# Gated linear recurrence: near-key products and their splitting moved from GpSimd to VectorE, decays of a level merged into one product

## The chip, the cores and the metric

The kernel runs on one core of a Trainium2 chip. The metric is the time of one execution on the device in microseconds (us); the median of several is compared. Smaller is better.

## The reference

Two pre-norm residual layers over 512 tokens of width 1024, all in float32. The first mixes tokens by a gated linear recurrence (8 heads, 128 keys and 128 values each), the second by sparse attention; each is followed by a feed-forward layer with a short convolution. The change touches the recurrence alone:

```python
forget = lb + (1.0 - lb) * sigmoid(f)          # per head, key dimension and token
k = (1.0 - lb) * sigmoid(-f)
log_f = log(maximum(forget, TINY))
...
b = cumsum(log_f)                              # within a chunk of 32
decay = exp(b[t] - b[s]) for s <= t
scores = einsum('bhtd,bhsd,bhtsd->bhts', q, k, decay)
o = scores @ i + (q * exp(b)) @ S              # S: state carried from chunk to chunk
S = exp(b_last) * S + (k * exp(b_last - b)) @ i
...
out = (rms_norm(o) * gate_norm * silu(g)) @ w_out
```

## The kernel before, in words

All activations lie transposed, features on the 128 partitions and tokens along the columns. Every float32 matrix product of a projection is made of three products of a high and a low part (`split`: ScalarE copies the high part, VectorE subtracts it for the low one; `mm3` issues the three). A projection to 128 features (`proj_T`) is 24 such products of 512 columns into one PSUM bank `pj`; its weights (1024 columns after loading) are split into `whi` and `wlo` (L143, L144).

The recurrence (42 to 304.5 us of the profile) runs head by head. `fq(h)` projects f and q, `gate(h)` projects g, and `recur(h)` does the head's recurrence. `recur` is a generator that is woven into the projections: each `yield` names how much projection work is to come before it goes on. So TensorE's order is written out by hand through these yields, while a scheduler orders the other engines when the program is built; every engine then takes its instructions in that fixed order.

`recur(h)` computes the 512 x 512 scores of a head by doubling. Distances of 0, 1 and 2 to 3 tokens are products of columns, w: `q * k` (512 columns, L489), one set of 256 (L487) and two of 256 (L493, tiles `w[1]`, `w[2]`). They are split into `wh`/`wl` and summed over the partitions by products with ones into three banks `pd`; then copied into `Sd` under masks (L528 to L534). Each level m = 4, 8, ... 256 multiplies blocks of m keys with the neighbouring m queries into a bank `pl` (L544 to L556), after which `decay(m)` multiplies queries of the second blocks (`qf`, L506) and keys of the first ones (`k`, L508) by decay factors out of a tree (`ftree`, L512), so that blocks of 2m are ready. Levels 32 and 64 use a packed copy of k (`kc`, L563). At the end the scores multiply the values (`po`), the result is normalised by ScalarE and GpSimd, transposed (`pt`), gated by g (L610) and split into `oh`/`ol`.

GpSimd has the 256-column products of w, their low parts `wl`, the product `g = g * gs` (L471) and two small operations on norms.

A head's level 256 stands in TensorE's order shortly before the next head's `pd`: this is what is called a seam below. "Decay 128" is the call `decay(128)`.

## Time and profile before

| what | value |
| --- | --- |
| median of 3 executions | 1307.05 us (1306.79 to 1308.17) |
| profiled execution | 1307.64 us, of which its span 1305.9 us |
| TensorE busy | 1260.3 us, 97% |
| VectorE, ScalarE, GpSimd busy | 858.9, 578.7, 185.7 us |
| mean granted clock of TensorE | 0.991 of full speed |

Busy time of matmuls overlaps from one to the next, so a high share does not say that TensorE runs at its peak; what counts is where it has gaps, what ends them, and at what clock it runs. GpSimd works mostly in the recurrence and in the attention.

### The profile page before, as it was taken

How to read it: one execution, taken by the hardware profiler on the slowest of the kernel's cores; microseconds unless marked ns; L12 is line 12 of the kernel's file. 1: busy time of each engine (PE TensorE's matmuls, PEld its weight loads, DVE VectorE, ACT ScalarE, POOL GpSimd, SP SyncE). 2: the span in 40 equal slices, each digit the busy share in tenths (PEclk: the TensorE clock that was granted, in tenths of full speed). 3: DMA queues.
4: the chain of work that ended last, by engine and by line, in shares of the span. 5: the costliest groups of instructions: out<-in, count | busy, mean ns of one | idle time of the engine just before them, and what ended most of it. 6: DMA issues, size and time to landing. Idle time of an engine off the chain costs nothing.

```text
span 1305.9 us, 15769 instructions
## 1 busy us (share of the span) xinstructions
PE 1260.3 (97%) x6054; PEld 1050.5 (80%) x6054; DVE 858.9 (66%) x1354; ACT 578.7 (44%) x980; POOL 185.7 (14%) x159
## 2 busy tenths in 40 slices
PE   9999899989999999999999979999999999999997
PEld 7788677778888888888887867898888888888887
DVE  7765988875677777762434799964677777772331
ACT  5434344444444444431325556873444444441430
POOL 3313233330000000000003385220000000000000
PEclk9989999999999999999999999999999999999999
DMA  6322221112333333333235221101333333332222
GB/s 194 100 63 67 63 66 49 49 50 84 93 97 97 97 97 98 97 97 97 89 98 145 65 65 34 49 2 53 107 99 98 97 97 97 97 97 97 82 80 65
DMA packets 171099, 109.90 MB, mean 84 GB/s; under 512 B 4832, under 2 KB 160400, under 8 KB 171024
## 3 DMA queue, kind: packets, MB, share of 16 engines
q1 hardware_dynamic: 170320, 108.31, 28.0%
q8 instruction: 47, 0.77, 0.2%
q10 hardware_dynamic: 704, 0.58, 0.2%
q14 instruction: 28, 0.23, 0.1%
HBM read 106.76 MB, written 2.12 MB: 83 GB/s over the span
## 4 chain that ended last, share of the span: by engine, by line
PE 83%; DVE 9%; POOL 3%; issue 2%; ACT 2%; DMA 0%; POOLq 0%; DVEq 0%; SPq 0%; ACTq 0%
PE pj L161 15%; PE pj L162 15%; PE pj L163 15%; PE px L161 8%; PE px L163 8%; PE px L162 8%; PE pav L911 2%; PE pl L544 1%; PE po L590 1%; DVE scs L750 1%; PE pn L162 1%; PE pn L161 1%; PE pn L163 1%; PE pl L852 1%; POOL wl L144 1%
## 5 line engine op out<-in xcount | busy, mean ns | idle before, releaser
L161 PE MATMUL pj<-x,whi 128*128 128x512 f32 (+1 forms) x1016 | 403.5, 397 | 0.0
L162 PE MATMUL pj<-x,whi 128*128 128x512 f32 (+1 forms) x1016 | 396.6, 390 | 0.0
L163 PE MATMUL pj<-x,wlo 128*128 128x512 f32 (+1 forms) x1016 | 396.6, 390 | 0.0
L144 DVE TENSOR_TENSOR wlo<-wr,whi 128x1024 fp32r<-128x1024 f32 (+2 forms) x184 | 228.1, 1240 | 165.0 <-ACT whi L143 162.5
L143 ACT ACTIVATE whi<-wr 128x1024 fp32r<-128x1024 f32 (+3 forms) x194 | 201.9, 1041 | 283.6 <-PE px L162 155.3
L163 PEld LDWEIGHTS pj<-x,wlo 128*128 128x128 f32 (+1 forms) x1016 | 190.9, 188 | 40.9
L161 PEld LDWEIGHTS pj<-x,whi 128*128 128x128 f32 (+1 forms) x1016 | 191.3, 188 | 39.4 <-issue 1.6
L162 PEld LDWEIGHTS pj<-x,whi 128*128 128x128 f32 (+1 forms) x1016 | 191.3, 188 | 38.9 <-issue 1.0
L161 PE MATMUL px<-ah,whi 128*128 128x512 f32 (+1 forms) x332 | 128.5, 387 | 0.0
L163 PE MATMUL px<-ah,wlo 128*128 128x512 f32 (+1 forms) x332 | 127.5, 384 | 0.0
L162 PE MATMUL px<-al,whi 128*128 128x512 f32 (+1 forms) x332 | 126.2, 380 | 0.0
L340 DVE TENSOR_TENSOR ub<-pj,rstd_r 128x512 f32<-128x512 f32 x88 | 60.6, 688 | 82.5 <-PE pj L163 77.6
L143 ACT ACTIVATE ah<-c 128x512 fp32r<-128x512 f32 x44 | 27.8, 631 | 116.0 <-DVE c L352 116.0
L163 PEld LDWEIGHTS px<-ah,wlo 128*128 128x128 f32 x332 | 62.3, 188 | 13.5
L162 PEld LDWEIGHTS px<-al,whi 128*128 128x128 f32 x332 | 62.3, 188 | 12.8
L343 ACT ACTIVATE c<-ub,convc 128x512 f32<-128x512 f32 x88 | 71.2, 809 | 2.4 <-DVE ub L340 1.6
L161 PEld LDWEIGHTS px<-ah,whi 128*128 128x128 f32 x332 | 62.4, 188 | 11.4
L345 DVE SCALAR_TENSOR_TENSOR c<-ub,convc,c 128x512 f32<-128x512 f32 x88 | 66.1, 752 | 3.0
L344 DVE SCALAR_TENSOR_TENSOR c<-ub,convc,c 128x512 f32<-128x512 f32 x88 | 65.6, 746 | 0.0
L350 ACT ACTIVATE c<-c 128x512 f32<-128x512 f32 x44 | 27.8, 632 | 80.7 <-DVE c L345 80.6
L321 POOL TENSOR_TENSOR rstd_c<-ms,half 128x2 f32<-128x2 f32 x2 | 1.4, 698 | 360.6 <-DVE ms L320 360.6
L712 POOL MEMSET vf<- 128x1536 f32 x1 | 1.4, 1382 | 354.0 <-PE px L163 354.0
(226 smaller groups left out, 1849.4 us busy)
## 6 DMA issues: line engine op xcount, KB each, us to landing
wr<-in_ffn_w_up_dram SPq DMA_DIRECT2D x88, 512.0 KB, 3.8
wr<-in_ffn_w_down_dram SPq DMA_DIRECT2D x41, 512.0 KB, 3.7
wr<-in_hgrn_w_in_dram SPq DMA_DIRECT2D x30, 512.0 KB, 4.1
wr<-in_dsa_w_in_dram SPq DMA_DIRECT2D x14, 512.0 KB, 3.7
wr<-in_hgrn_w_out_dram SPq DMA_DIRECT2D x8, 512.0 KB, 3.5
wr<-in_dsa_w_out_dram SPq DMA_DIRECT2D x8, 512.0 KB, 3.8
back<-Z SPq DMA_DIRECT2D x4, 512.0 KB, 4.4
out_dram<-hT SPq DMA_DIRECT2D x4, 512.0 KB, 4.2
```

The lines of the kernel that those rows point to most:

```text
L143: nc.scalar.activation(dst_h, src, AF.Copy)
L144: lo.tensor_tensor(dst_l, src, dst_h.bitcast(F32), op=ALU.subtract)
L161: nc.tensor.matmul(o, ah, bh, start=start, stop=False)
L162: nc.tensor.matmul(o, ah, bl, start=False, stop=False)
L163: nc.tensor.matmul(o, al, bh, start=False, stop=stop)
L340: nc.vector.tensor_tensor(u[:, 2:], o, rows(), op=ALU.mult)
L343: nc.scalar.activation(c, u[:, 2:], AF.Identity, scale=cc[2], bias=cc[3])
L344: nc.vector.scalar_tensor_tensor(c, u[:, 1:T + 1], cc[1], c, op0=ALU.mult, op1=ALU.add)
L345: nc.vector.scalar_tensor_tensor(c, u[:, 0:T], cc[0], c, op0=ALU.mult, op1=ALU.add)
L350: nc.scalar.activation(g, g, AF.Silu)
L544: nc.tensor.matmul(pl[:, ts_], k[:, ts_], qf[:, ts_], start=True, stop=True)
L911: nc.tensor.matmul(o[:, :256], vf[:, s, kv, c], px[:, e, s * 256:s * 256 + 256], start=e == 0 and s == 0, stop=False)
```

## The change

In each head's `recur`:

- the 256-column products of w go from GpSimd to VectorE. The two sets for distances 2 and 3 become one product of 512 columns. All lie in one tile `w` of 1280 columns;
- `w` is split by one copy on ScalarE and one subtraction on VectorE, where there were three copies on ScalarE and three subtractions on GpSimd;
- `qf` and `k` lie in one tile `qk`, and one product on VectorE of 512 columns (`turned(m)` by `factors(.., m)`) replaces the two of 256 columns at the first split and at each level;
- the factor 1 - lb of k is moved to q, where it joins the multiplication by the norm, so k's own multiplication goes; the scale and bias of f go from VectorE to ScalarE;
- `decay(m)` and `kc` are issued ahead of the yield that follows the level's products instead of behind it;
- the buffer counts of the tiles `tmp`, `f` and `q` go from 3 to 2.

GpSimd keeps `g = g * gs` and the two small operations.

```diff
--- before.py
+++ after.py
@@ -202,7 +202,7 @@
         if n == 0:
             nc.scalar.activation(sqa, hT[:, n, :], AF.Square)
         else:
-            sq = pool.tile([P, T], F32, name="sq", tag="tmp", bufs=3) if pool else nrm.tile([P, T], F32, name="sq", bufs=1)
+            sq = pool.tile([P, T], F32, name="sq", tag="tmp", bufs=2) if pool else nrm.tile([P, T], F32, name="sq", bufs=1)
             nc.scalar.activation(sq, hT[:, n, :], AF.Square)
             (nc.gpsimd if pool else nc.vector).tensor_tensor(sqa, sqa, sq, op=ALU.add)
 
@@ -443,55 +443,66 @@
     def fq(h):
         hs = slice(h, h + 1)
         pf = yield from proj_T(w_in, D + h * P)
-        f = hw.tile([P, T], F32, name="f", bufs=3)
-        k = hw.tile([P, T], F32, name="k", bufs=3)
+        f = hw.tile([P, T], F32, name="f", bufs=2)
+        qk = hw.tile([P, 2, T], F32, name="qk", bufs=3)
 
         def forget():
-            fr = hw.tile([P, T], F32, name="fr", tag="tmp", bufs=3)
+            fr = hw.tile([P, T], F32, name="fr", tag="tmp", bufs=2)
             nc.vector.tensor_tensor(fr, pf, rows(), op=ALU.mult)
             nc.scalar.activation(f, fr, AF.Sigmoid)
-            nc.scalar.activation(k, fr, AF.Sigmoid, scale=-1.0)
-            nc.vector.tensor_scalar(f, f, omlb[:, hs], lb[:, hs], op0=ALU.mult, op1=ALU.add)
+            nc.scalar.activation(qk[:, 1, :], fr, AF.Sigmoid, scale=-1.0)
+            nc.scalar.activation(f, f, AF.Identity, scale=omlb[:, hs], bias=lb[:, hs])
             nc.vector.tensor_scalar(f, f, TINY, None, op0=ALU.max)
-            nc.vector.tensor_scalar(k, k, omlb[:, hs], None, op0=ALU.mult)
             if h == 0:
                 values_out()
 
         pq = yield from proj_T(w_in, h * P, hook={3: forget})
-        q = hw.tile([P, T], F32, name="q", bufs=3)
-        nc.vector.tensor_tensor(q, pq, rows(), op=ALU.mult)
-        heads[h] = [q, f, k]
+        q = hw.tile([P, T], F32, name="q", bufs=2)
+
+        nc.vector.scalar_tensor_tensor(q, pq, omlb[:, hs], rows(), op0=ALU.mult, op1=ALU.mult)
+        heads[h] = [q, f, qk]
 
     def gate(h):
         pg = yield from proj_T(w_in, 3 * D + h * P)
         g = hw.tile([P, T], F32, name="g")
         nc.vector.tensor_tensor(g, pg, rows(), op=ALU.mult)
-        gs = hw.tile([P, T], F32, name="gs", tag="tmp", bufs=3)
+        gs = hw.tile([P, T], F32, name="gs", tag="tmp", bufs=2)
         nc.scalar.activation(gs, g, AF.Sigmoid)
         nc.gpsimd.tensor_tensor(g, g, gs, op=ALU.mult)
         heads[h].append(g)
 
     def recur(h):
-        q, f, k = heads[h]
+        q, f, qk = heads[h]
+        qf, k = qk[:, 0, :], qk[:, 1, :]
         Sd = hw.tile([P, TT, P], F32, name="Sd")
         S1 = hw.tile([P, 2, P], F32, name="S1")
         S2 = hw.tile([P, 2, 256], F32, name="S2")
 
 
-        qf = hw.tile([P, T], F32, name="qf")
         nc.vector.tensor_tensor(qf, q, f, op=ALU.mult)
-        w = [hw.tile([P, T], F32, name=f"w{i}", tag="tmp", bufs=3) for i in range(3)]
+        w = hw.tile([P, 1280], F32, name="w", bufs=1)
         q2, k2, f2 = (a.rearrange("p (n two) -> p n two", two=2) for a in (qf, k, f))
         q4, k4 = (a.rearrange("p (n four) -> p n four", four=4) for a in (qf, k))
         ftree = hw.tile([P, T], F32, name="ftree")
-        nc.gpsimd.tensor_tensor(w[1][:, :256], k2[:, :, 0], q2[:, :, 1], op=ALU.mult)
+        nc.vector.tensor_tensor(w[:, :512], q, k, op=ALU.mult)
+        nc.vector.tensor_tensor(w[:, 512:768], k2[:, :, 0], q2[:, :, 1], op=ALU.mult)
+
+        def turned(m):
+
+            nb = T // (2 * m)
+            return bass.AP(tensor=qk.tensor, offset=qk.offset + m, ap=[list(qk.ap[0]), [T - m, 2], [2 * m, nb], [1, m]])
+
+        def factors(fv, m):
+
+            nb = T // (2 * m)
+            return bass.AP(tensor=fv.tensor, offset=fv.offset, ap=[list(fv.ap[0]), [1, 2], [2, nb], [0, m]])
+
+        nc.vector.tensor_tensor(turned(1), turned(1), factors(f, 1), op=ALU.mult)
         nc.vector.tensor_tensor(ftree[:, :256], f2[:, :, 0], f2[:, :, 1], op=ALU.mult)
-        nc.vector.tensor_tensor(w[0], q, k, op=ALU.mult)
-        nc.vector.tensor_tensor(q2[:, :, 1], q2[:, :, 1], f2[:, :, 0], op=ALU.mult)
-        nc.vector.tensor_tensor(k2[:, :, 0], k2[:, :, 0], f2[:, :, 1], op=ALU.mult)
-        for i, o in ((0, w[1][:, 256:]), (1, w[2][:, :256])):
-            nc.gpsimd.tensor_tensor(o.rearrange("p (n two) -> p n two", two=2), q4[:, :, 2:],
-                                    k4[:, :, i:i + 1].to_broadcast([P, P, 2]), op=ALU.mult)
+        nc.vector.tensor_tensor(w[:, 768:].rearrange("p (i n two) -> p i n two", i=2, two=2),
+                                q4[:, None, :, 2:].to_broadcast([P, 2, P, 2]),
+                                k4[:, :, :2].rearrange("p n i -> p i n")[:, :, :, None].to_broadcast([P, 2, P, 2]),
+                                op=ALU.mult)
         trees = [ftree[:, :256], 256]
 
         def decay(m):
@@ -500,24 +511,17 @@
                 return
             ft, off = trees
             nb = T // (2 * m)
-            fv = ft.rearrange("p (n two) -> p n two", two=2)
-            qv = qf.rearrange("p (n two m) -> p n two m", two=2, m=m)
-            kv = k.rearrange("p (n two m) -> p n two m", two=2, m=m)
-            nc.vector.tensor_tensor(qv[:, :, 1, :], qv[:, :, 1, :],
-                                    fv[:, :, 0:1].to_broadcast([P, nb, m]), op=ALU.mult)
-            nc.vector.tensor_tensor(kv[:, :, 0, :], kv[:, :, 0, :],
-                                    fv[:, :, 1:2].to_broadcast([P, nb, m]), op=ALU.mult)
+            nc.vector.tensor_tensor(turned(m), turned(m), factors(ft, m), op=ALU.mult)
             if 4 * m < T:
+                fv = ft.rearrange("p (n two) -> p n two", two=2)
                 nft = ftree[:, off:off + nb]
                 nc.vector.tensor_tensor(nft, fv[:, :, 0], fv[:, :, 1], op=ALU.mult)
                 trees[:] = [nft, off + nb]
 
-        wp = []
-        for i, n in enumerate((512, 512, 256)):
-            wh = hw.tile([P, n], F32R, name=f"wh{i}", bufs=1)
-            wl = hw.tile([P, n], F32R, name=f"wl{i}", bufs=1)
-            split(wh, wl, w[i][:, :n], nc.gpsimd)
-            wp.append((wh, wl))
+        wh = hw.tile([P, 1280], F32R, name="wh", bufs=1)
+        wl = hw.tile([P, 1280], F32R, name="wl", bufs=1)
+        split(wh, wl, w)
+        wp = [(wh[:, c], wl[:, c]) for c in (slice(0, 512), slice(512, 1024), slice(1024, 1280))]
         yield START if h else 6.0
         decay(2)
         pd = [bank("pd")[:, :n] for n in (512, 512, 256)]
@@ -555,13 +559,13 @@
                 for i in range(2):
                     nc.tensor.matmul(pl[:, i * 256:(i + 1) * 256], k[:, i * P:(i + 1) * P],
                                      qf[:, 256:], start=True, stop=True)
-            yield LEV
             decay(m)
             if m in (16, 32):
 
                 kc = hw.tile([P, 256], F32, name="kc")
                 nc.scalar.activation(kc.rearrange("p (n m) -> p n m", m=2 * m),
                                      k.rearrange("p (n two m) -> p n two m", two=2, m=2 * m)[:, :, 0, :], AF.Copy)
+            yield LEV
             if m in LEVELS:
                 nc.vector.copy_predicated(
                     Sd, masks[:, LEVELS.index(m), None, :].to_broadcast([P, TT, P]), plv)
```

TensorE's rows stand in the same order in both programs, but for the tiles' names and the line numbers. VectorE's order moves. The first place is the seam of one of the heads 4 to 6, from the weight split ahead of level 64's decay to the next weight split. Before (the three-dimensional shapes are those of the decays, 128x2x128 is decay 128; `ol` belongs to the head before, `g` with L468 to this head's gate):

```order
L144 TENSOR_TENSOR wlo<-wr,whi 128x1024
L506 TENSOR_TENSOR qf<-qf,ftree 128x4x64
L506 TENSOR_TENSOR qf<-qf,ftree 128x128x2
L610 SCALAR_TENSOR_TENSOR g<-pt,cols,g 128x512
L508 TENSOR_TENSOR k<-k,ftree 128x128x2
L144 TENSOR_TENSOR ol<-g,oh 128x512
L468 TENSOR_TENSOR g<-pj,rstd_r 128x512
L506 TENSOR_TENSOR qf<-qf,ftree 128x2x128
L508 TENSOR_TENSOR k<-k,ftree 128x2x128
L144 TENSOR_TENSOR wlo<-wr,whi 128x1024
```

and in the changed program, where L514 is the merged decay (its last two numbers tell the level, 128x2x4x64 is decay 64), L500 the first split's, L502 the product of 512 columns, L614 the old L610:

```order
L144 TENSOR_TENSOR wlo<-wr,whi 128x1024
L500 TENSOR_TENSOR qk<-qk,f 128x2x256
L514 TENSOR_TENSOR qk<-qk,ftree 128x2x4x64
L502 TENSOR_TENSOR w<-qk 128x512
L614 SCALAR_TENSOR_TENSOR g<-pt,cols,g 128x512
L514 TENSOR_TENSOR qk<-qk,ftree 128x2x128x2
L468 TENSOR_TENSOR g<-pj,rstd_r 128x512
L144 TENSOR_TENSOR wl<-w,wh 128x1280
L144 TENSOR_TENSOR ol<-g,oh 128x512
L514 TENSOR_TENSOR qk<-qk,ftree 128x2x2x128
L144 TENSOR_TENSOR wlo<-wr,whi 128x1024
```

Decay 128 stood behind `g` and now stands behind `g`, the 1280-column `wl` and `ol`; two decays of 256 columns became one of 512 each time.

The second place is the first two heads, from the second head's q (L462) to the first head's decay 4. Before:

```order
L462 TENSOR_TENSOR q<-pj,rstd_r 128x512
L482 TENSOR_TENSOR qf<-q,f 128x512
L528 TENSOR_TENSOR Sd<-pd,ident 128x512
L489 TENSOR_TENSOR w_550<-q,k 128x512
L490 TENSOR_TENSOR qf<-qf,f 128x256
L491 TENSOR_TENSOR k<-k,f 128x256
L532 COPY_PREDICATED Sd<-pairs,pd 128x256
L144 TENSOR_TENSOR wlo<-wr,whi 128x1024
L534 COPY_PREDICATED Sd<-pairs,pd 128x128x2
L506 TENSOR_TENSOR qf<-qf,ftree 128x64x4
L534 COPY_PREDICATED Sd<-pairs,pd 128x128x2
L508 TENSOR_TENSOR k<-k,ftree 128x64x4
```

and in the changed program, where L532 to L538 are the copies into `Sd`:

```order
L462 SCALAR_TENSOR_TENSOR q<-pj,omlb,rstd_r 128x512
L518 TENSOR_TENSOR ftree<-ftree 128x8
L144 TENSOR_TENSOR wlo<-wr,whi 128x1024
L482 TENSOR_TENSOR qk<-q,f 128x512
L487 TENSOR_TENSOR w<-q,qk 128x512
L488 TENSOR_TENSOR w<-qk 128x256
L532 TENSOR_TENSOR Sd<-pd,ident 128x512
L500 TENSOR_TENSOR qk<-qk,f 128x2x256
L536 COPY_PREDICATED Sd<-pairs,pd 128x256
L502 TENSOR_TENSOR w<-qk 128x512
L538 COPY_PREDICATED Sd<-pairs,pd 128x128x2
L514 TENSOR_TENSOR qk<-qk,ftree 128x2x64x4
```

The weight split now stands ahead of the second head's products, the products L488 and L502 stand among them, and decay 4 of the first head (128x2x64x4) stands before the last pair copy instead of around it.

## Rows read from the trace of the kernel before

**Rows 1.** The page's chain that ended last: shares of the span by engine.

```profile
PE 83%; DVE 9%; POOL 3%; issue 2%; ACT 2%; DMA 0%; POOLq 0%; DVEq 0%; SPq 0%; ACTq 0%
```

**Rows 2.** Table by stretch: length, busy of the engines, TensorE's granted clock, DMA.

```profile
42.00:118.00 76.00, 71.90 (x361) 59.93 (x360) 52.40 (x97) 31.73 (x73) 17.97 (x17) 0.96 0.26 77
118.00:154.00 36.00, 30.05 (x149) 23.89 (x147) 31.66 (x53) 13.07 (x25) 15.60 (x13) 1.00 0.20 59
154.00:241.10 87.10, 79.03 (x426) 66.50 (x426) 73.56 (x131) 38.65 (x97) 31.78 (x27) 0.98 0.19 55
241.10:304.50 63.40, 59.77 (x322) 50.31 (x323) 42.04 (x69) 25.55 (x72) 16.35 (x15) 0.97 0.18 57
304.50:338.00 33.50, 33.50 (x147) 26.90 (x146) 23.70 (x31) 16.23 (x23) 0.19 (x4) 1.00 0.31 90
```

**Rows 3.** TensorE's timeline: start, duration in us, what, idle before and its releaser.

```profile
54.10 0.39 PE L163 MATMUL pj<-x,wlo 128*128 128x512 f32 x1
...
66.16 1.19 PE L544 MATMUL pl<-qf,k 128*128 128x128 f32 x4 [4.10 <-DVE k L508]
...
134.93 1.16 PE L544 MATMUL pl<-qf,k 128*128 128x128 f32 x8 [1.70 <-DVE k L508]
...
208.19 0.39 PE L162 MATMUL pj<-x,whi 128*128 128x512 f32 x1
...
208.41 0.40 PE L163 MATMUL pj<-x,wlo 128*128 128x512 f32 x1
...
211.11 0.67 PE L556 MATMUL pl<-qf,k 128*128 128x256 f32 x2 [2.30 <-DVE k L508]
...
276.42 0.82 PE L544 MATMUL pl<-qf,k 128*128 128x128 f32 x5 [1.56 <-DVE k L508]
```

**Rows 4.** Table by stretch, three short ones behind gaps of TensorE.

```profile
66.10:72.10 6.00, 5.94 (x18) 4.63 (x19) 6.00 (x8) 1.87 (x3) 3.47 (x3) 0.52 0.24 63
211.10:216.10 5.00, 4.99 (x16) 4.14 (x17) 3.45 (x5) 0.60 (x1) 2.13 (x1) 0.66 0.38 108
242.00:246.00 4.00, 4.00 (x14) 3.21 (x13) 3.03 (x5) 0.60 (x1) 1.29 (x1) 0.57 0.41 134
```

**Rows 5.** VectorE's timeline at the seam between two heads.

```profile
198.83 0.69 DVE L462 TENSOR_TENSOR q<-pj,rstd_r 128x512 f32<-128x512 f32 x1 [0.36 <-PE pj L163]
...
200.71 1.35 DVE L489 TENSOR_TENSOR w<-q,k 128x512 f32<-128x512 f32 x1
...
202.65 1.87 DVE L144 TENSOR_TENSOR wlo<-wr,whi 128x1024 fp32r<-128x1024 f32 x1
...
204.45 1.51 DVE L506 TENSOR_TENSOR qf<-qf,ftree 128x256 f32<-128x256 f32 x1
...
209.61 0.68 DVE L468 TENSOR_TENSOR g<-pj,rstd_r 128x512 f32<-128x512 f32 x1
...
210.21 0.41 DVE L506 TENSOR_TENSOR qf<-qf,ftree 128x256 f32<-128x256 f32 x1
...
210.54 0.42 DVE L508 TENSOR_TENSOR k<-k,ftree 128x256 f32<-128x256 f32 x1
...
210.88 1.22 DVE L144 TENSOR_TENSOR wlo<-wr,whi 128x1024 fp32r<-128x1024 f32 x1
```

**Rows 6.** GpSimd's timeline, at the same seam and at a later one.

```profile
203.41 2.27 POOL L144 TENSOR_TENSOR wl<-w,wh 128x512 fp32r<-128x512 f32 x1
...
271.19 1.28 POOL L471 TENSOR_TENSOR g<-g,gs 128x512 f32<-128x512 f32 x1 [2.33 <-ACT gs L470]
```

**Rows 7.** Groups by form, 42 to 305 us: count, busy us, mean ns, idle before.

```profile
L610 DVE SCALAR_TENSOR_TENSOR g<-pt,cols,g 128x512 f32<-128x512 f32 x7 | 5.2, 745 | 5.0 <-PE pt L607 3.8 <-POOL g L471 1.2
...
L534 DVE COPY_PREDICATED Sd<-pairs,pd 128x256 f32<-128x256 uint8 x16 | 11.7, 728 | 0.9
...
L143 ACT ACTIVATE wh<-w 128x512 fp32r<-128x512 f32 x16 | 10.1, 633 | 32.8 <-POOL w L493 16.5 <-DVE w L489 16.3
...
L143 ACT ACTIVATE whi<-wr 128x1024 fp32r<-128x1024 f32 x29 | 30.5, 1051 | 38.9 <-PE pj L162 35.3 <-PE pn L163 3.6
```


## The prediction

> **What bounds the kernel now.** I read the chain of waits first: TensorE carries 83% of it, VectorE 9% and GpSimd 3% [rows 1]. The reader should see that only those last shares, and what they do to TensorE's clock, can be won. The table by stretch tells where they lie: between 304.50 and 338.00 TensorE has no gap, while the recurrence, 42 to 304.5 us, has gaps of 4.10, 5.95, 8.07 and 3.63 us [rows 2], some 21.8 in all. The mean granted clock is below 1 in three of those four stretches.
>
> TensorE's own rows show what the gaps are. It waits for VectorE's decay products: 4.10 us at 66.16, 1.70 at 134.93, 2.30 at 211.11, 1.56 at 276.42 [rows 3]. A gap costs a little more than its idle time: a projection row lasts 0.40, but the next one can start 0.22 to 0.23 after its start (208.19, 208.41) [rows 3], so behind the row at 208.41 the next was due at 208.64, and each gap costs its idle plus 0.17.
>
> The clock is the second cost. [...] At full clock the same work would have taken 0.48 x 5.94 = 2.9, 0.34 x 5 = 1.7 and 0.43 x 4 = 1.7 us less: 6.3 us. The stretch from 118 to 154 has 5.95 us of shorter gaps, the one of 1.70 among them, and a clock of 1.00 [rows 2, 3].
>
> Last, why VectorE is late. At the seam between two heads, 198.83 to 211, a 512-wide product takes 1.35 us, the weight split 1.87, a 256-wide decay 1.51; a little later the same split takes 1.22, a 512-wide row 0.68 and the same decay 0.41 [rows 5]. The slow ones lie under GpSimd's operations: one of these runs from 203.41 to 205.68, and the decay that began at 204.45 ends at 205.96, 0.28 behind it [rows 6]. So the two engines take turns, and the three rows lose 0.67 + 0.65 + 1.10 = 2.4 us.
>
> **The change, part by part.** TensorE's order is the same row for row, so time can only come from its waits and its clock. VectorE's steps between starts, without blocking: 0.60 us for 512 columns, 0.33 for 256, 1.14 for the 1024-wide split (1.22 less the overlap of 0.08) [rows 5], 0.67 for a scalar_tensor_tensor out of PSUM and 0.65 for a predicated copy [rows 7], each less 0.08. The 1280-wide split of the near-key products is not in the trace. Bounds: 1.22 (the 1024 row) and 1.22 + 0.68 = 1.90 (two operations); by the slope between 512 and 1024, 1.05 ns a column, it is 1.49, step 1.41. A merged decay (512 columns in a four-step pattern, factors repeated) is not there either: not under 0.41, and 1.22 if it took two passes. The strided and repeated 256-wide ones take 0.41 already, half a plain 512-wide row and its fixed part, so I take 0.69, step 0.60. ScalarE's 1280-wide copy lies between 1.05 (the 1024 row) and 1.68 (the three copies now) [rows 7]; by the slope 1.25. Its new scale-and-bias pass over f lies between 0.63 (a 512-wide copy) and 1.05 [rows 7]; VectorE, which has a weight split to do meanwhile, then waits 0.5 to 0.9 for f, and the third level has 0.9 in hand, so I count nothing; without that cover it is up to 0.9 a head. The multiplication of k goes. The smaller buffer counts of tmp, f and q cost nothing: their older tile is read long before the next is written.
>
> *Seams of heads 3 to 6 (three).* VectorE's order there becomes q, qk, decay 32, w, w, weight split, first split decay, decay 64, w, gated head, decay 2, g, wl, ol, decay 128. From 198.83, when q's projection is done: 0.67 + 3 x 0.60 + 0.33 + 1.14 + 3 x 0.60 + 0.67 + 2 x 0.60 + 1.41 + 0.60 = 9.62, so decay 128 could start at 208.45 and end at 209.14. With the 0.15 from the last decay's end to TensorE's start now (210.54 + 0.42 to 211.11) [rows 3, 5] the product of 211.11 would start at 209.3: 1.8 a seam. But GpSimd keeps g = g x gs. ScalarE starts wh when w is done, 204.7, then oh, S1, whi and gs: about 1.16 + 0.54 + 0.35 + 1.00 + 0.63, from copies of 1.25, 0.63, 0.42 (256 columns, by the slope) and 1.05 [rows 7] less the overlap, puts the end at 208.4, so GpSimd is ready just as ol ends at 208.45. Who waits already gets the turn: GpSimd's operation of 203.41 sat out VectorE's weight split (to 204.52) and then went ahead of the decay of 204.45 [rows 5, 6]. It is a matter of less than 0.1 us; I give GpSimd the turn. Its product alone takes 1.28 [rows 6], and a 512-wide row then ends some 0.55 behind it (0.28 for the 256-wide one): 210.3, the TensorE product at 210.4. Gain 0.7 a seam, three times: 2.0. Gaps of 2.0 stay: the 1.41 of wl and the 0.60 of ol now stand ahead of decay 128, work that GpSimd did beside the path or that came behind it.
>
> *Heads 2 and 3 (118 to 154).* Gaps 5.95 in five waits, cost 5.95 + 5 x 0.17 = 6.8. By the same steps wl is ready 0.4 before its product, decays 4 and 8 end within 0.1 of TensorE's demand, and the later ones have 0.4 or more; in the first of these seams no ol or wl stands before decay 128. Left: 0.2. Gain 6.6.
>
> *Heads 0 and 1.* The second head's q projection ends at 54.49 [rows 3]. From 54.6 VectorE has q, a tree product (0.1), weight split, qk, w, w, Sd, first decay, pair copy, w, pair copy, decay 4: 0.67 + 0.1 + 1.14 + 0.60 + 0.60 + 0.33 + 0.60 + 0.60 + 0.65 + 0.60 + 0.65 = 6.5, then 0.69 + 0.15: 62.0, where TensorE now waits from 62.06. Behind it wl, g on GpSimd and six copies of two heads crowd VectorE: I count a wait of 0.3 there, 0.45 at level 8, and 1.75 where the copy kc of level 64 comes behind decay 32. Gain 4.10 + 0.17 - 2.5 = 1.8.
>
> *Head 7 (to 304.5).* Idle 3.6 in five waits, cost 4.5. Here pd follows directly on the m = 128 product, so it waits for wl, by the seam's steps some 1.75; the 1.56 at 276.42 shrinks to 0.7 (decay 4 was 0.4 early, but g's turn costs VectorE 1.1); 0.3 at kc stays. Gain 1.75.
>
> *Clock.* The gaps left are 2.0 and shorter. The 1.70 at 134.93 kept 1.00, and so did its neighbours, so I count no fall: 6.3.
>
> Sum: 2.0 + 6.6 + 1.8 + 1.75 + 6.3 = 18.5 us. The profiled execution took 1307.64 (span 1305.9 and 1.74 around it), 0.6 above the median of 1307.05; from the median: **1288.5 us**.
>
> **Rivals.**
> *The last decay is first.* If GpSimd comes after decay 128 at the seams, each gives 1.8 instead of 0.7, and head 7 0.6 more: 18.5 + 3.4 + 0.6 = 22.5, 1284.5. [...]
> *The clock falls at the seams all the same.* Of the three seams of 154 to 241.1 (8.07 us of gaps, of 2.3 and a small one each) two lost 1.7 each; gaps of 2.0 are nearer to those than to the 1.7 that kept their clock. One fall 1290.2, two 1292.
> *No change.* VectorE becomes the bound with work that ran beside it. By the steps it has some 21 us a head (15 x 0.60, 2 x 0.67, 3 x 1.14, 1.41, 6 x 0.65, 1.0 in 256-wide and 0.9 in tree products) in a period of 29 (87.1 for three [rows 2]). It would have to lose 7 us a head in waits of its own: 1306.
> *Slower: the merged pattern takes two passes*, 1.22 for 0.69. A seam has five such operations up to decay 128: +2.65, so the product of 211.11 comes at 212.0 without any turn of GpSimd's. Three seams +2.6, a third clock fall +1.7; in heads 2 and 3 all but 1.5 us of the gaps come back; heads 0 and 1 lose 1.2 more: 1311. It decides from 0.36 us extra an operation, where a seam gains nothing even undisturbed. Against it: the 0.41 of strided, repeated rows [rows 5].
>
> **How the numbers follow.** Forecast 0.36, decay first 0.30, clock 0.24, no change 0.05, slower 0.05. The time is the forecast's. Low: the undisturbed seams, with heads 0 and 1 free of their 2.5 us of waits: 1281. High: two falls of clock and 5 us of late steps, as when head 0's fall stays too and a wait of 2 us appears: 1297. That leaves out about 0.15. Within 0.2% (2.6 us, about what a measurement here can tell from no change) lies the third rival: same 0.05, slower 0.05, faster 0.90.
>
> **What would show it.** Right: no VectorE row of 1.3 to 1.9 us for 256 or 512 columns except beside g; merged decays of 0.69, wl of 1.49; no gap of 4 us near 62; 118 to 154 almost without gaps; at each seam one gap ended by decay 128, of 1.0 or 2.0 as g's turn falls. Wrong: merged decays over 1 us, gaps above 2.3 at the seams, new waits of ScalarE's copies, or half clock behind gaps under 1.7.

## The result, and the profile after

The changed kernel takes **1284.34 us** (median of four executions, 1283.52 to 1284.62), the kernel before beside it on the same chip 1307.61 (1306.79 to 1308.38): a ratio of 0.982, 95% interval 0.980 to 0.984, or 23 us less. The forecast was 1288.5 in a range of 1281 to 1297; the time fell on the rival "the last decay is first", 1284.5. One execution of one experiment (1580 us, one row added behind decay 128) ran at a granted clock of 0.75 and is left out of its median. Line numbers from here on are those of the changed kernel, in which the merged decay is L514, the weight split's low part wl is L144, and TensorE's level products are L548 (levels to 16), L552 (32 and 64) and L560 (256, L556 in the kernel before).

First the page of the profiled execution: the span, the busy time by engine, and the chain's shares by engine, which answer to [rows 1].

```profile
span 1282.8 us, 15611 instructions
...
PE 1251.3 (98%) x6054; PEld 1045.4 (81%) x6054; DVE 840.9 (66%) x1298; ACT 580.5 (45%) x972; POOL 132.1 (10%) x111
...
PE 85%; DVE 8%; ACT 3%; issue 2%; POOL 1%; DMA 0%; POOLq 0%; SPq 0%; DVEq 0%; ACTq 0%
```

Next the table by stretch, with the stages of [rows 2] at their new times (the same to within a few rows): length, TensorE's busy time and rows, granted clock, DMA share, GB/s.

```profile
42.00:112.00 70.00, 69.72 (x364) 1.00 0.28 84
112.00:143.00 31.00, 30.81 (x155) 1.00 0.24 68
143.00:221.40 78.40, 75.09 (x420) 1.00 0.22 61
221.40:281.30 59.90, 57.77 (x322) 1.00 0.19 60
281.30:315.00 33.70, 33.70 (x149) 1.00 0.32 92
```

Length less busy time is what TensorE stood idle: 0.28, 0.19, 3.31 and 2.13 us, where it was 4.10, 5.95, 8.07 and 3.63 [rows 2]. That is 21.75 before and 5.91 now, 15.8 us gained. The clock is 1.00 in all five stretches; the three falls of [rows 4] cost 0.48 x 6 + 0.34 x 5 + 0.43 x 4 = 6.3 (1.00 less the clock, by the length) and are gone. Together 22.1 of the 23.1 us by which the span shrank; the last 1.0 lies within what two-decimal clocks and single executions can tell.

TensorE's waits between 36 and 320 us show what is left: the tile waited for and who writes it, us in total, how often, the longest.

```profile
PE pl L560 <- DVE qk L514: 3.4, 3, 1.1
PE pd L530 <- DVE wl L144: 1.5, 1, 1.5
PE pl L552 <- ACT kc L566: 0.8, 2, 0.5
PE pl L548 <- DVE qk L514: 0.2, 1, 0.2
```

The three waits of 1.1 are one at each seam, ended by decay 128; the 1.5 is the last head's, ended by wl. The gap of 4.10 at 66.16 and the 1.70 and 1.56 of [rows 3] have no answer here. Now one seam: first VectorE's timeline (start, length), then the GpSimd row and the TensorE row that belong to it.

```profile
192.03 1.48 DVE L144 TENSOR_TENSOR wl<-w,wh 128x1280 fp32r<-128x1280 f32 x1
193.43 0.69 DVE L144 TENSOR_TENSOR ol<-g,oh 128x512 fp32r<-128x512 f32 x1
194.03 0.69 DVE L514 TENSOR_TENSOR qk<-qk,ftree 128x512 f32<-128x512 f32 x1
194.63 1.22 DVE L144 TENSOR_TENSOR wlo<-wr,whi 128x1024 fp32r<-128x1024 f32 x1
```

```profile
194.03 2.98 POOL L471 TENSOR_TENSOR g<-g,gs 128x512 f32<-128x512 f32 x1 [12.71 <-ACT gs L470]
```

```profile
194.77 1.13 PE L560 MATMUL pl<-qk 128*128 128x256 f32 x4 [1.13 <-DVE qk L514]
```

No VectorE row is stretched here as those of [rows 5] were: 0.69 for decay 128, where the decay there took 1.51. GpSimd's g starts at 194.03, in the same hundredth as decay 128, and it is g's row that is longer than elsewhere: 2.98, where [rows 6] has 1.28. The 1.70 between them is close to the time from 194.03 to the end of the weight split at 195.85, so I read it as g standing back through both rows. The trace shows only starts and lengths; below, an engine asks where its row starts, and it has the turn where its row keeps its usual length and the other engine's row does not. The other two seams look the same (g at 167.32 and 220.74, 2.98 each).

### The profile page after: what moved, and what is told of

It is laid out like the page before. It is cut to its first block, busy times and chain, and to the rows that moved or that the text cites. A ratio compares the mean times of both kernels' runs of the same rounds, so it can differ in the third digit from the quotient of the medians.

```text
span 1282.8 us, 15611 instructions
## 1 busy us (share of the span) xinstructions
PE 1251.3 (98%) x6054; PEld 1045.4 (81%) x6054; DVE 840.9 (66%) x1298; ACT 580.5 (45%) x972; POOL 132.1 (10%) x111
## 4 chain that ended last, share of the span: by engine, by line
PE 85%; DVE 8%; ACT 3%; issue 2%; POOL 1%; DMA 0%; POOLq 0%; SPq 0%; DVEq 0%; ACTq 0%
PE pj L161 16%; PE pj L162 16%; PE pj L163 16%; PE px L161 9%; PE px L163 9%; PE px L162 8%; PE pav L915 2%; PE pl L548 1%; PE po L594 1%; DVE scs L754 1%; PE pl L856 1%; PE pt L904 1%; DVE scs L770 1%; DVE wlo L144 1%; PE pn L162 1%
## 5 line engine op out<-in xcount | busy, mean ns | idle before, releaser
L144 DVE TENSOR_TENSOR wlo<-wr,whi 128x1024 fp32r<-128x1024 f32 (+2 forms) x184 | 225.0, 1223 | 164.9 <-ACT whi L143 162.8
L514 DVE TENSOR_TENSOR qk<-qk,ftree 128x512 f32<-128x512 f32 x56 | 39.7, 710 | 16.3 <-PE pl L548 6.9
L144 DVE TENSOR_TENSOR al<-c,ah 128x512 fp32r<-128x512 f32 x44 | 30.5, 692 | 29.3 <-ACT ah L143 29.3
```

What stands on the lines that cost most here:

```text
L144: lo.tensor_tensor(dst_l, src, dst_h.bitcast(F32), op=ALU.subtract)
L514: nc.vector.tensor_tensor(turned(m), turned(m), factors(ft, m), op=ALU.mult)
```

## The experiments

Two things had to be told apart. **What carries the gain:** theory 1, GpSimd's operations, which held VectorE up and made TensorE wait for slow splits; theory 2, VectorE's smaller work (merged decays, no multiplication of k, f's scale on ScalarE); theory 3, the earlier place of decay and kc. Theory 4 is about the clock: its falls go where no gap of more than 2 us is left. **What the forecast got wrong at the seams:** theory A, who has waited gets the turn; theory B, VectorE's next row goes first.

**Near-key work back on GpSimd, all else of the change kept.**

```diff
-        nc.vector.tensor_tensor(w[:, 512:768], ...)
+        nc.gpsimd.tensor_tensor(w[:, 512:768], ...)
-        nc.vector.tensor_tensor(w[:, 768:].rearrange(...
+        nc.gpsimd.tensor_tensor(w[:, 768:].rearrange(...
-        split(wh, wl, w)
+        split(wh, wl, w, nc.gpsimd)
```

> The changed kernel with the 256- and 512-wide near-key products and the weight split's low part (1280) back on GpSimd; merged decays, the k multiplication folded into q, and the decay ahead of the yield stay. Theory 1 (the gain is GpSimd's work leaving: its operations make VectorE lose turns, and TensorE waits for its slow split): most of the 23 us comes back, about 1303 (1297 to 1309), with TensorE waiting for wl from POOL and VectorE rows of 1.3 to 1.9 us where 0.68 stood. Theory 2 (the gain is the smaller VectorE work by merged decays and folded multiplications): stays below 1291.

Measured 1312.08, ratio to the kernel before 1.004 (1.0025 to 1.0055): not the 1303 of theory 1 but slower than the kernel before, and nowhere near theory 2's 1291. TensorE's waits, the longest:

```profile
PE pl L560 <- DVE qk L514: 9.9, 4, 3.2
PE pd L530 <- POOL wl L144: 6.1, 3, 2.5
PE pl L548 <- DVE qk L514: 5.7, 2, 5.4
```

GpSimd's timeline, and then VectorE's, at one seam:

```profile
208.16 2.90 POOL L144 TENSOR_TENSOR wl<-w,wh 128x1280 fp32r<-128x1280 f32 x1 [1.39 <-ACT wh L143]
```

```profile
208.63 2.98 DVE L144 TENSOR_TENSOR ol<-g,oh 128x512 fp32r<-128x512 f32 x1 [1.13 <-ACT oh L143]
```

The 1280-wide split is one operation of 2.90 on GpSimd, and VectorE's `ol`, which takes 0.69 at 193.43 of the changed kernel, takes 2.98 here: it starts 0.47 behind the split's start and ends 0.55 behind its end. The kernel before had three smaller splits here (one of 2.27 at 203.41, two of 2.18 together from 206.62), and VectorE's rows ended in between, at 205.96, 207.64 and 208.30; that the one large tile is what makes this run slower than the kernel before is argued from these rows, not shown by a run of its own (the products and the order differ too). The clock fell six times here (0.57 over 62 to 70 and 128 to 132, 0.72 over 182 to 188, for three of them).

**The kernel before, with nothing but the move.**

```diff
-        nc.gpsimd.tensor_tensor(w[1][:, :256], ...)
+        nc.vector.tensor_tensor(w[1][:, :256], ...)
         for i, o in ((0, w[1][:, 256:]), (1, w[2][:, :256])):
-            nc.gpsimd.tensor_tensor(o.rearrange(...
+            nc.vector.tensor_tensor(o.rearrange(...
-            split(wh, wl, w[i][:, :n], nc.gpsimd)
+            split(wh, wl, w[i][:, :n])
```

> The kernel before with only one edit: the three near-key products and the three weight-split low parts are issued on VectorE instead of GpSimd, in the old tiles of 512, 512 and 256 columns; separate decays, the k multiplication, f on VectorE and the old place of the yield stay. Theory 1: most of the gain, about 1289 (1285 to 1294). Theory 2: VectorE gets 3 us more work in each head and nothing is taken from it, so no gain, 1300 to 1310. Theory 4 (the clock falls go where no gap of more than 2 us is left): clock 1.00 in every window if the gaps are below 2 us.

Measured 1282.24, ratio 0.981 (0.979 to 0.983), below theory 1's range. All of the gain, and 2 us more than the whole change gives (its interval overlaps that of the change, so the 2 us are not settled). The longest wait is 1.4, and the clock is 1.00 throughout the recurrence, as theory 4 has it. The page's busy times and TensorE's waits:

```profile
PE 1252.6 (98%) x6054; PEld 1046.7 (82%) x6054; DVE 851.8 (66%) x1402; ACT 577.0 (45%) x980; POOL 133.3 (10%) x111
```

```profile
PE pl L544 <- DVE k L508: 3.9, 4, 1.4
PE pl L548 <- ACT kc L563: 0.6, 1, 0.6
```

VectorE is busy for 10.9 us more than in the changed kernel, and none of it is seen by TensorE. Against the kernel before its busy time even fell, from 858.9 to 851.8, although it took over GpSimd's work: the stretching of its rows had cost more than that work does. Theory 2 falls: merging the decays saves busy time on an engine that had room.

There is no wait for wl and none at the seams. At the last head VectorE's three splits, and the first product that reads them:

```profile
240.51 1.62 DVE L144 TENSOR_TENSOR wl<-w,wh 128x512 fp32r<-128x512 f32 x3
```

```profile
244.03 0.39 PE L526 MATMUL pd<-wl,ones_r 128*128 128x512 f32 x1
```

All three are written 1.9 us before TensorE reads the first. They stand ahead of the gated head's row and of decay 2 in VectorE's order here; in the changed kernel the single wl stands behind both. So the waits that the changed kernel still has, 1.13 at each seam and 1.46 at the last head, come with its order as well as with its single tile, and no run tells the two apart.

**Only the splits, and only the products.** The same edit in two halves: the last pair of lines alone, and the first two pairs alone.

> The kernel before with only the three low parts of the weight split issued on VectorE; the three near-key products stay on GpSimd. Theory 1, if GpSimd's time is what counts: the splits are some 3.2 of 5.3 us of GpSimd's work in a head, so about 60% of the gain, 1292 (1288 to 1297). Rival (a threshold: once the gaps are under 2 us the clock falls go and nearly all of it is there): below 1287. Other rival (the products are what matters, since everything waits for them): above 1300.

> The kernel before with only the near-key products of 256, 256 and 256 columns issued on VectorE; the three low parts stay on GpSimd. Theory 1, if GpSimd's time is what counts: about 40% of the gain, 1298 (1293 to 1303). Rival (threshold): below 1287. Other rival (the splits are what matters): above 1303.

Splits alone 1298.29 (ratio 0.993, 0.991 to 0.995), products alone 1293.97 (0.989, 0.988 to 0.991): gains of 9 and 14 us, which add to 23 of the 25 of both. Neither alone gives nearly everything; and they are not shares by GpSimd's time either, where the splits had the larger part. But they add up only because of the clock. TensorE between 36 and 320 us (length, busy time and rows, clock), first with the splits alone on VectorE, then with the products alone:

```profile
36.00:320.00 284.00, 266.28 (x1389) 0.99 0.23 66
```

```profile
36.00:320.00 284.00, 269.67 (x1417) 1.00 0.23 68
```

The idle time is 17.7 and 14.3 us, where the kernel before has 21.8 and both together leave 4.8 in the same stretch: gains of 4.0 and 7.4 for 17.0. Half of the work on GpSimd still makes most of the gaps. With the splits alone two falls of the clock stay (0.72 over 62 to 68 and over 229 to 235), with the products alone none in the profiled execution, so much of the clock's 6.3 us is won twice. What is left, TensorE's waits with the splits alone on VectorE:

```profile
PE pl L552 <- DVE qf L506: 10.7, 5, 2.4
PE pl L544 <- DVE k L508: 6.1, 4, 3.3
```

and with the products alone there:

```profile
PE pl L544 <- DVE k L508: 6.9, 4, 3.8
PE pl L556 <- DVE k L508: 5.4, 3, 1.8
PE pd L526 <- POOL wl L144: 1.2, 1, 1.2
```

The products stand at the head of the chain: while they ran on GpSimd a decay could not overwrite qf and k before they had been read (in the kernel before VectorE stood idle for 0.73 ahead of the decay of 206.69, until GpSimd's product had ended). How much of the gain is stretched rows and how much such waits for GpSimd's own results, no run separates. With the splits moved alone, the rows at 193.91 (w, 1.35 for 0.69) and 195.85 (weight split, 1.87 for 1.22) are still stretched beside them.

**Decays given out as two operations again.**

```diff
-        nc.vector.tensor_tensor(turned(1), turned(1), factors(f, 1), op=ALU.mult)
+        for i in range(2):
+            nc.vector.tensor_tensor(turned(1)[:, i], turned(1)[:, i], factors(f, 1)[:, i], op=ALU.mult)
...
-            nc.vector.tensor_tensor(turned(m), turned(m), factors(ft, m), op=ALU.mult)
+            for i in range(2):
+                nc.vector.tensor_tensor(turned(m)[:, i], turned(m)[:, i], factors(ft, m)[:, i], op=ALU.mult)
```

> The changed kernel with each merged decay given out as two operations again (256 columns for q, 256 for k); the scheduler then puts the gate's product behind the decay of level 128. Two 256-wide steps of 0.33 to 0.4 take 0.06 to 0.2 longer than the merged 0.60. Theory 1: about 1286 (1284.5 to 1288). Theory 2: a third of the gain or more goes back, 1292 or more.

Measured 1285.67, ratio 0.984 (0.982 to 0.985), as theory 1 had it: the merge is worth 1.3 us by the medians, within the scatter. It is not the merge's price alone, since the order moved with it: three seam waits of 1.1 became 0.6, and a new one of 2.28 at 142.53 is a turn that GpSimd's g did get ahead of decay 128:

```profile
140.12 1.64 POOL L471 TENSOR_TENSOR g<-g,gs 128x512 f32<-128x512 f32 x1 [20.38 <-ACT gs L470]
```

```profile
140.56 1.82 DVE L516 TENSOR_TENSOR qk<-qk,ftree 128x256 f32<-128x256 f32 x2
```

The two halves of the decay took 1.82, where 0.75 is usual (0.41 and a step of 0.34).

**Decay and kc behind the yield again.**

```diff
-            decay(m)
+            yield LEV
+            decay(m)
...
-            yield LEV
             if m in LEVELS:
```

> The changed kernel with the decay and the copy kc behind the yield again, as before the change. Theory 1: VectorE has room, so the order costs little: 1284 to 1286. Theory 3 (the earlier decay is what takes the waits in the middle of a head away): the waits for kc and for the decays come back, some 0.5 to 1 us in each of six heads: 1288 to 1291.

Measured 1286.43, ratio 0.984 (0.983 to 0.986): 2.1 us over the change, between the two expectations. The waits for kc come back (3.3 us in seven, the longest 0.8), but decay 128 now ends earlier (2.1 us of waits at L560 for 3.4). Theory 3 holds for a tenth of the gain, and even that is not settled, since the intervals overlap.

**GpSimd asks earlier.** The gate in two halves, so that its first product is ready before decay 128 could start.

```diff
-        nc.scalar.activation(gs, g, AF.Sigmoid)
-        nc.gpsimd.tensor_tensor(g, g, gs, op=ALU.mult)
+        for c in (slice(0, 256), slice(256, 512)):
+            nc.scalar.activation(gs[:, c], g[:, c], AF.Sigmoid)
+            nc.gpsimd.tensor_tensor(g[:, c], g[:, c], gs[:, c], op=ALU.mult)
```

> The changed kernel with the gate's sigmoid (ScalarE) and its product g (GpSimd) cut into two halves of 256 columns, so that GpSimd asks some 0.35 us earlier, while VectorE is still inside ol, the row ahead of decay 128; VectorE's program is the same. Theory A (who has waited longest gets the turn): half of g runs ahead of decay 128 at the three seams, which adds about 0.66 us to each, 1286 to 1287. Theory B (VectorE's next operation always goes first when its rows lie back to back): seams unchanged at 1.13 us, 1284 to 1285.

Measured 1283.51, ratio 0.982 (0.980 to 0.983), 0.5 under theory B's range: theory B at the seams. The timelines of VectorE and of GpSimd at a seam:

```profile
192.71 0.69 DVE L144 TENSOR_TENSOR ol<-g,oh 128x512 fp32r<-128x512 f32 x1
193.31 0.68 DVE L515 TENSOR_TENSOR qk<-qk,ftree 128x512 f32<-128x512 f32 x1
193.91 1.22 DVE L144 TENSOR_TENSOR wlo<-wr,whi 128x1024 fp32r<-128x1024 f32 x1
```

```profile
193.10 3.33 POOL L472 TENSOR_TENSOR g<-g,gs 128x256 f32<-128x256 f32 x2 [12.50 <-ACT gs L471]
```

GpSimd could start at 193.10, 0.21 before decay 128, and still both VectorE rows behind ol ran unstretched; its two rows end at 196.43, behind them. The three seam gaps stayed at 1.13.

**The gate's product on VectorE.**

```diff
-        nc.gpsimd.tensor_tensor(g, g, gs, op=ALU.mult)
+        nc.vector.tensor_tensor(g, g, gs, op=ALU.mult)
```

> The changed kernel with the product g issued on VectorE (512 wide, a step of 0.60), behind decay 128 at the seams; no GpSimd row is left beside the recurrence. Theory A (GpSimd's g still costs turns: the seams, and 1.1 us ahead of the copy kc of the last head): 1281.5 to 1283.5, the wait of 0.54 at kc of the last head gone. Theory B (g on GpSimd already costs VectorE nothing at the seams): 1283.5 to 1285.5.

Measured 1282.50, ratio 0.981 (0.979 to 0.982). At the seams theory B again: with no g on GpSimd the same three gaps of 1.13 stand. In the last head theory A: the wait of 0.54 at kc is gone. In the changed kernel that wait came from a turn that GpSimd did get; its row and the VectorE rows there:

```profile
258.01 1.23 DVE L144 TENSOR_TENSOR wlo<-wr,whi 128x1024 fp32r<-128x1024 f32 x1 [0.17 <-ACT whi L143]
...
259.15 1.77 DVE L514 TENSOR_TENSOR qk<-qk,ftree 128x512 f32<-128x512 f32 x1
```

```profile
258.58 1.79 POOL L471 TENSOR_TENSOR g<-g,gs 128x512 f32<-128x512 f32 x1 [9.30 <-ACT gs L470]
```

Asked at 258.58, in the middle of a weight split, GpSimd went ahead of the decay of 259.15, which took 1.77.

**Longer seam gaps.** Rows that alter nothing between decay 128 and the product of level 256.

```diff
             decay(m)
+            if m == 128:
+                for _ in range(2):
+                    nc.vector.tensor_tensor(k, k, k, op=ALU.max)
```

> The changed kernel with one 512-wide VectorE row that alters nothing (the maximum of k with itself) between decay 128 and TensorE's product of level 256, in all heads; a weight row of 1.14 lies ahead of it. Each of the three seam gaps of 1.13 us becomes about 2.9. Theory 1 (the clock falls only behind a long gap, and the gaps are now short enough): the falls come back behind these gaps, 2 to 3 us each, together with the gaps themselves 1294 to 1298. Rival (the clock fell for another reason, GpSimd's load or the order): no falls, the gaps alone, 1289 to 1291.

The kernel that ran had two such rows, not the one of its expectation, so 3.5 us was to be expected of a gap by its own steps (1.13 + 1.14 + 2 x 0.60). Measured 1309.98, ratio 1.002 (1.001 to 1.003): with two small rows in each head the whole gain is lost. A seam in TensorE's timeline:

```profile
210.93 2.04 PE L560 MATMUL pl<-qk 128*128 128x256 f32 x4 [4.63 <-DVE qk L565]
```

4.63, since by the rows' lengths GpSimd's g now ran between the two added rows: at the seam before this one g starts at 175.11 and ends at 178.65, and the two added rows, from 176.85 on, took 2.35 together and not 1.28. Four gaps of this kind (4.27, then three of 4.63) and four falls of the clock (0.57 over 148 to 152, 0.72 over 178 to 184 and 242 to 248, 0.66 over 208 to 218). With one row in place of the two:

```diff
             if m == 128:
-                for _ in range(2):
-                    nc.vector.tensor_tensor(k, k, k, op=ALU.max)
+                nc.vector.tensor_tensor(k, k, k, op=ALU.max)
```

> The changed kernel with exactly one row (the maximum of k with itself, 512 wide) between decay 128 and the product of level 256; the run with such rows before this one had two. The weight row of 1.14 and the step of 0.6 make each seam gap about 2.9 us (1.13 + 1.14 + 0.60). Theory 1 (the clock falls behind gaps of over 2 us): gaps of 5.3 together and three falls of some 2 us, 1295 to 1298. Rival (no falls at 2.9): 1289.5 to 1291.

Measured 1297.29, ratio 0.992 (0.990 to 0.994), within theory 1's range. Gaps of 2.53, 2.96, 2.96 and 2.96, 8.0 us more than the changed kernel's; the clock in the stretches behind them, and behind the 1.46 for wl at 257.45:

```profile
143.00:149.00 6.00, 5.68 (x30) 1.00 0.29 87
172.00:178.00 6.00, 6.00 (x23) 0.72 0.30 87
202.00:208.00 6.00, 6.00 (x34) 1.00 0.32 90
230.00:236.00 6.00, 5.59 (x19) 0.72 0.26 91
258.00:262.00 4.00, 4.00 (x13) 0.57 0.02 4
```

Three falls of 1.7 us each (6 x 0.28, 4 x 0.43): 8.0 + 5.0 = 13, for 12.95 in the medians (11.7 between the two profiled executions). The long gaps bring the falls back, as theory 4 has it, but not every one: two of these four kept 1.00, and one fall came behind a gap of 1.46.

**The low part later**, so that decay 128 stands ahead of wl at the seams.

```diff
-        split(wh, wl, w)
+        nc.scalar.activation(wh, w, AF.Copy)
...
-        yield START if h else 6.0
+        yield 3.5
+        nc.vector.tensor_tensor(wl, w, wh.bitcast(F32), op=ALU.subtract)
+        yield START - 3.5 if h else 6.0 - 3.5
```

> The changed kernel with the weight split's low part wl issued 3.5 us of pacing later than the high part, so that at the seams decay 128 stands ahead of wl on VectorE. Theory 1 (TensorE waits at the seam for what stands ahead of decay 128, and wl is not needed until behind it): the three gaps of 1.13 go, pd waits at most 0.2 instead; the last head's wait for wl (1.46) may grow by 0.5: 1280.5 to 1282.5. Rival (wl is itself next in line, the wait only moves to pd): 1284 to 1285.5.

Measured 1285.05, ratio 0.983 (0.981 to 0.984): the time lies in the rival's range, but by neither mechanism. TensorE's one long wait, and the stretch behind it:

```profile
246.33 0.50 PE L532 MATMUL pd<-wl,ones_r 128*128 128x512 f32 x1 [2.75 <-DVE wl L526]
```

```profile
246.00:252.00 6.00, 5.67 (x20) 0.72 0.27 90
```

All three seam gaps are gone, as expected, and pd does not wait there. But the last head, where pd has nothing between it and wl, waits 2.75 for 1.46 and loses 1.6 (5.67 x 0.28) to the clock.

**Both remedies, the last head left alone.**

```diff
-        nc.gpsimd.tensor_tensor(g, g, gs, op=ALU.mult)
+        nc.vector.tensor_tensor(g, g, gs, op=ALU.mult)
...
-        split(wh, wl, w)
+        nc.scalar.activation(wh, w, AF.Copy)
...
-        yield START if h else 6.0
+        late = 3.5 if 0 < h < NH - 1 else 0
+        if late:
+            yield late
+        nc.vector.tensor_tensor(wl, w, wh.bitcast(F32), op=ALU.subtract)
+        yield START - late if h else 6.0
```

> The changed kernel with wl issued late in heads 1 to 6 only, so that decay 128 stands ahead of it at the seams and the last head keeps its order, and with the product g on VectorE. If the two causes add: the seam gaps (3 x 1.13) and the kc wait of the last head (0.54) go, pd of the last head keeps 1.46: 1280 to 1281.5. Rival (g's 0.6 on VectorE, now behind the late wl and ahead of the copies of Sd, makes the levels of the next head late): 1282.5 or more.

Measured **1279.05** (five executions), ratio 0.978 (0.977 to 0.980), below both kernels and 1 us under its expected range. Against the move alone (0.979 to 0.983) it is not clear of the scatter. TensorE's waits between 36 and 330, all that are left:

```profile
PE pd L534 <- DVE wl L528: 1.5, 1, 1.5
PE pl L556 <- ACT kc L570: 0.3, 1, 0.3
```

## Why the prediction was right in its mechanism and 4 us too slow

The mechanism holds: GpSimd's operations made VectorE late; without them most of the gaps go, and with the gaps the falls of the clock. The move alone gives all of the gain, and giving the work back takes all of it away. By the forecast's own terms:

- **Seams, forecast 2.0: the step that failed.** Idle time went from 8.07 to 3.31, 4.8 gained. "Who waits already gets the turn" and "I give GpSimd the turn" are wrong here: g was ready as decay 128 started, and even 0.21 before it in the halved gate, and VectorE went first at all three seams of both runs. The prediction's precedent, the GpSimd operation of 203.41, had asked in the middle of a weight split, 1.04 before the decay that it went ahead of; and where g asked 0.44 before decay 128, in the run with the decays as two operations, it did get the turn, and the gap was 2.28. So the prediction had when g is ready right to 0.1 us and the rule for the turn wrong. Without g's turn the steps came out: from the start of q (184.29) to L560 (194.77) 9.74 + 0.69 + 0.05 = 10.48 us, forecast 9.62 + 0.69 + 0.15 = 10.46. At the seams this is the rival "the last decay is first".
- **Heads 2 and 3, forecast 6.6**: 5.95 to 0.19 in idle time, 5.8; the 0.17 charged to each of five waits on top cannot be told: over the whole recurrence 17 waits became 8, which would be 1.5 us, and only 1.0 is left over by idle time and clock.
- **Heads 0 and 1, forecast 1.8**: 4.10 to 0.28, 3.8. Of the waits of 0.3, 0.45 and 1.75 that were counted as left, 0.28 is there in all. They were put down to wl, g and six copies crowding VectorE; g's row at 66.53 (2.22 long) gave way to a decay and then ran beside two copies into Sd (67.51 out of pd, 68.11 out of pl), which took 0.70 and 0.75, where 0.69 and 0.73 are usual.
- **Head 7, forecast 1.75**: 3.63 to 2.13, 1.5. pd waits 1.46 for wl as said (1.75). With the move alone it is zero, with three tiles and wl further ahead in the order; which of the two does it is not shown. Here GpSimd did get a turn, at 258.58.
- **Clock, forecast 6.3**: 6.3. The gaps left are 1.46 and shorter, and no stretch is below 1.00.
- **Operations never seen before.** VectorE's merged decay 0.69 to 0.71 (taken 0.69), wl 1.49 (1.49), ScalarE's wh 1.28 (1.25), its scale and bias over f 0.80 (0.63 to 1.05); VectorE waited 3.0 us for f in all eight heads together, off TensorE's path. The rival of two passes is out with the first of these.

The idle time left was forecast too high by 3.7 us (12.15 gained by the terms without the clock, 15.8 measured): nearly all of the error of 4.2. The seams make 2.8 of the 3.7 and heads 0 and 1 another 2.0, while the other heads gave 1.0 less than forecast. So the rival's time was met to 0.2 us partly by luck: by its own terms the seams were to give 5.4 (4.8 measured) and head 7 2.35 (1.5), and heads 0 and 1 made up for that. The low end of the range, by its own terms 22.5 + 2.5 below 1307.05, is 1282.0 and not 1281.

One thing the prediction did not say, since it costed the change as a whole: its parts are worth very different sums. Of 23 us the move has all; undoing the merged decays or the earlier decay and kc costs 1.3 and 2.1 by the medians, neither clear of the scatter. All that the change has beside the move together gives nothing (1284.34 against 1282.24), since its order also brings the waits at the seams and at the last head.

## What to carry to other kernels

Where rows of an engine that feeds the critical path are longer beside those of an engine off it (here 1.51 for 0.41 and 1.87 for 1.22 [rows 5]), price the second engine's work by the rows that it stretches, not by its own length: taking it away can be worth more than the receiving engine's added work, as long as that engine has idle time (here VectorE's busy time fell from 858.9 to 851.8 with GpSimd's near-key work added). A large tile saved VectorE little (1.49 for the single wl, 1.62 for the three splits), but on GpSimd it was one row of 2.90, beside which a VectorE row of 0.69 took 2.98, and its consumer waited for the whole of it (pd for up to 2.5 there). Before merging operations to save busy time, look whether the busy engine is the one that is waited for; then move what is not yet needed behind what is, as the late wl did, and leave out the place where it is needed at once.

## What the runs showed of the hardware

**Where rows of VectorE and GpSimd overlapped, the turn did not always go to the one that asked first.** GpSimd's product, ready before the next VectorE row, went ahead of it at 258.58 in the changed kernel (asked 0.57 before the decay of 259.15, which took 1.77 for 0.69), and there in the row of 141.34 too (0.93 before the weight split of 142.27, which took 2.32 for 1.22). It stood back at 193.10 in the halved gate (0.21 before the decay of 193.31, which took 0.68). At 175.11 in the kernel with two added rows it let three VectorE rows in succession pass (175.11 and 175.71, which took 0.69 and 1.22, and 176.85) and ran ahead of the fourth: the two rows from 176.85 on end at 179.20, 0.55 behind g's end at 178.65, as the row of 2.98 in the run with the near-key work back on GpSimd ended 0.55 behind its split. How long it has waited does not decide, then: by this reading it lost the turn at 176.85 after 1.74 us. Nor does how shortly before a row it asks: with the splits alone moved, g asked at 202.56, only 0.14 before the `ol` of 202.70, and went ahead of it (`ol` took 1.78 for 0.69, g 1.38). In the kernel before, a split of GpSimd's asked at 66.56, 0.33 before the decay of 66.89, and went ahead too (the decay took 1.49 for 0.41). At the seam of the changed kernel shown above, where it had let two rows pass, g's 1.28 of work fits only from about 195.73 to its end at 197.01, an estimate: there VectorE stood idle from 195.85 to 196.41 and then copied out of pd in its usual 0.69. What decides the first turn stays open; a sum should carry both ends.

**The clock fell behind long gaps, but not behind all.** Over the recurrence in the kernel before, the changed one and the twelve of the experiments, TensorE had 26 gaps of 2.2 us or more, and behind (or in) 18 of them the granted clock fell, to between 0.50 and 0.54 in the lowest stretch of 2 us; of 33 gaps between 1.0 and 1.8 one (1.46 at 257.45 with one row added) was followed by such a fall. Equal gaps differ: 2.96 at 171.83 fell, 2.96 at 201.91 in the same execution did not, and with the products alone moved a gap of 3.76 at 65.13 kept 1.00. A fall cost 1.5 to 3 us by the estimates above (busy time times what the clock lacked). The counts are of one profiled execution of each kernel. So the gaps explain that falls come and go, not which one comes.
